# Decoder trunk on one core: half of the down projection's low weight halves formed by ScalarE and an accumulating DMA

## The chip, the cores and the metric

The kernel runs on one core of one Trainium2 chip. The metric is the device time of one execution in microseconds (us); three runs of the kernel before gave 2397.7 to 2398.99 us, median 2398.13 us. TensorE, VectorE, ScalarE, GpSimd and SyncE stand in the profile as PE, DVE, ACT, POOL and SP.

## The reference

Two identical layers are applied to x, one sequence of 256 tokens with 2048 channels, float32:

```python
for l in range(DEPTH):                       # DEPTH = 2
    h = rms_norm(x, mix_norm_w[l])
    x = x + hybrid_mixer(h, w_in[l], ..., w_out[l])
    h = rms_norm(x, ffn_norm_w[l])
    x = x + swiglu(h, w_gate[l], w_up[l], w_down[l])
return rms_norm(x, final_norm_w)

def swiglu(h, w_gate, w_up, w_down):         # 2048 x 5632, 2048 x 5632, 5632 x 2048
    return (jax.nn.silu(h @ w_gate) * (h @ w_up)) @ w_down
```

The mixer runs three groups of heads (mLSTM, forgetting attention, gated DeltaNet) between two projections. All weights are float32 and each is used once per execution.

## The kernel before

The weights lie in HBM as units of 128 x 1024 float32 (512 KB), 410 of them per layer, in the order in which the program uses them. For each unit, `unit` (L112 to L125) has SP load it into a tile `raw` (three buffers), has ACT write a copy rounded to the fp32r format into `whi` (L123), and has DVE write the rest, `raw - whi`, into `wlo` (L124). `whi` and `wlo` have four buffers each. A product of float32 accuracy is then three fp32r matmuls: high by high, high by low, low by high.

The feed-forward part, `ffn`, cuts its 5632 hidden columns into three parts of 16, 16 and 12 blocks of 128. In each part, for every block, `block_a` multiplies one gate block and one up block (two units each); first all matmuls with `whi` (L157, tiles `pg` and `pu`), then those with `wlo` (L161), so that all four `wlo` buffers are held until the end of a block. Then comes the down projection of the part: `block_b` goes through 32 units (24 in the third part), and each unit serves 12 matmuls of 512 columns in the order `whi`, `wlo`, `whi` for two groups of tokens (L184, L185, L186, tile `dn`). In the third part the last 512 output columns are taken in two stretches of 256 columns, the very last of them in the last layer by `block_b_halves` (L199 to L201). Over both layers there are 176 down units in six entries from gate and up to down.

The order on each engine's queue is set by the scheduler of the tile framework, from its own estimate of the times; buffers are handed on by semaphores. POOL has little to do: powers for the norms (L211), some of the convolution (L472, L475) and memsets. It issues no DMA.

Of the kernel before, what the change touches and what calls it, by code (L numbers as in the profile page):

```python
# [15 lines left out]
AF = mybir.ActivationFunctionType  # L16
ALU = mybir.AluOpType
AX = mybir.AxisListType
MUL, ADD, SUB, MAX = ALU.mult, ALU.add, ALU.subtract, ALU.max
# [40 lines left out]
def tile_trunk(ctx: ExitStack, tc: tile.TileContext, x: bass.AP, wu: bass.AP, prm: bass.AP,  # L60
               cst: bass.AP, fnw: bass.AP, out: bass.AP, depth: int, units: list):
    nc = tc.nc
    act, dve, pe, pool = nc.scalar, nc.vector, nc.tensor, nc.gpsimd
# [33 lines left out]
    def f32(ap):  # L97
        return ap.bitcast(F32)
# [5 lines left out]
    def fetch(desc):  # L104
        u, n = len(units), desc[-1] * desc[-2]
        units.append(desc)
        raw = wp.tile([P, 1024], F32, tag="raw", name="raw", bufs=3)[:, :n]
        nc.sync.dma_start(out=raw, in_=wu[u][:, :n])
        return raw
# [4 lines left out]
    def unit(desc):  # L114

        raw = fetched.pop(desc) if desc in fetched else fetch(desc)
        n = desc[-1] * desc[-2]
        whi = wp.tile([P, 1024], F32R, tag="whi", name="whi")[:, :n]
        wlo = wp.tile([P, 1024], F32R, tag="wlo", name="wlo")[:, :n]
        halves = 2 if desc == FIRST else 1  # L120
        for i in range(halves):
            c = slice(i * n // halves, (i + 1) * n // halves)
            act.activation(out=whi[:, c], in_=raw[:, c], func=AF.Copy)  # L123
            dve.tensor_tensor(out=wlo[:, c], in0=raw[:, c], in1=f32(whi[:, c]), op=SUB)  # L124
        return whi, wlo  # L125


# [20 lines left out]
    def block_a(l, cols, hs):  # L148


        los = []
        for mat, col, ps in cols:
            for half in range(2):
                whi, wlo = unit(("a", l, mat, col, half * 8, 8, P))
                los.append(wlo)
                for i in range(8):
                    pe.matmul(ps, whi[:, i * P:(i + 1) * P], hs[half * 8 + i][2], start=(half + i == 0), stop=False)  # L157
        for n, (mat, col, ps) in enumerate(cols):
            for half in range(2):
                for i in range(8):  # L160
                    pe.matmul(ps[:, :S], los[2 * n + half][:, i * P:(i + 1) * P], hs[half * 8 + i][0],  # L161
                              start=False, stop=(half == 1 and i == 7))
# [9 lines left out]
    def block_b(l, mat, col, pst, hs, k0, kts, first, last, w=512):  # L172

        n = 1024 // w
        for j in range(0, kts, n):
            whi, wlo = unit(("b", l, mat, col, k0 + j, min(n, kts - j), w))
            for i in range(min(n, kts - j)):
                hhi, hlo = hs[j + i][:2]
                w1, w2 = whi[:, i * w:(i + 1) * w], wlo[:, i * w:(i + 1) * w]
                st = first and j + i == 0  # L180
                en = last and j + i == kts - 1
                for t in range(2):
                    sl = slice(t * P, (t + 1) * P)
                    pe.matmul(pst[t][:, :w], hhi[:, sl], w1, start=st, stop=False)  # L184
                    pe.matmul(pst[t][:, :w], hhi[:, sl], w2, start=False, stop=False)  # L185
                    pe.matmul(pst[t][:, :w], hlo[:, sl], w1, start=False, stop=en)  # L186

    def block_b_halves(l, mat, col, pst, hs, k0, kts, w):

        n = 1024 // w  # L190
        ws = []
        for j in range(0, kts, n):
            whi, wlo = unit(("b", l, mat, col, k0 + j, n, w))
            ws += [(whi[:, i * w:(i + 1) * w], wlo[:, i * w:(i + 1) * w]) for i in range(n)]
        for t in range(2):
            sl = slice(t * P, (t + 1) * P)
            for j, (w1, w2) in enumerate(ws):
                hhi, hlo = hs[j][:2]
                pe.matmul(pst[t][:, :w], hhi[:, sl], w1, start=(j == 0), stop=False)  # L199
                pe.matmul(pst[t][:, :w], hhi[:, sl], w2, start=False, stop=False)  # L200
                pe.matmul(pst[t][:, :w], hlo[:, sl], w1, start=False, stop=(j == kts - 1))  # L201
# [725 lines left out]
```

## Time and profile before

| | |
|---|---|
| median of three runs | 2398.13 us |
| the profiled execution's own time | 2399.22 us |
| its span in the trace | 2397.4 us |
| PE busy | 2382.9 us, 99% of the span, granted clock 0.999 |
| DVE busy | 1477.3 us, 62% |
| ACT busy | 1194.7 us, 50% |
| POOL busy | 77.2 us, 3% |
| DMA | 436.11 MB, mean 182 GB/s, SP's queue 55.6% of 16 engines |

Busy time of PE says that a matmul is under way, not that it runs at its peak; but an engine that is busy for 99% of the span leaves almost no gaps for others to fill. The page's chain that ended last gives PE 97% of the span. `dn<-wlo,hid` means an instruction that writes the tile `dn` from `wlo` and `hid`; L124 is line 124 of the kernel. In the rows further down, a bracket with an arrow names what ended the idle time of the engine before the row.

### The profile page before, as it was taken

How to read it: one execution, taken by the hardware profiler on the slowest of the kernel's cores; microseconds unless marked ns; L12 is line 12 of the kernel's file. 1: busy time of each engine (PE TensorE's matmuls, PEld its weight loads, DVE VectorE, ACT ScalarE, POOL GpSimd, SP SyncE). 2: the span in 40 equal slices, each digit the busy share in tenths (PEclk: the TensorE clock that was granted, in tenths of full speed). 3: DMA queues.
4: the chain of work that ended last, by engine and by line, in shares of the span. 5: the costliest groups of instructions: out<-in, count | busy, mean ns of one | idle time of the engine just before them, and what ended most of it. 6: DMA issues, size and time to landing. Idle time of an engine off the chain costs nothing.

```text
span 2397.4 us, 34530 instructions
## 1 busy us (share of the span) xinstructions
PE 2382.9 (99%) x13344; PEld 2081.5 (87%) x13344; DVE 1477.3 (62%) x2246; ACT 1194.7 (50%) x1879; POOL 77.2 (3%) x107
## 2 busy tenths in 40 slices
PE   9999999999999999999999999999999999999998
PEld 8888888888888888888898888889888888888887
DVE  5896655566655655466558865565665556655665
ACT  6754554555434454444567545454544344544544
POOL 0220000000000000000003000000000000000000
PEclk9999999999999999999999999999999999999999
DMA  6554555465555656555655545454656555565564
GB/s 223 170 172 132 162 164 187 165 194 192 193 195 176 196 190 201 185 182 196 191 173 176 176 130 164 164 178 161 193 196 195 194 183 186 194 209 193 185 200 161
DMA packets 120885, 436.11 MB, mean 182 GB/s; under 512 B 13584, under 2 KB 14352, under 8 KB 120720
## 3 DMA queue, kind: packets, MB, share of 16 engines
q1 hardware_dynamic: 120160, 432.75, 55.6%
q8 instruction: 104, 1.70, 0.3%
q10 hardware_dynamic: 560, 1.15, 0.1%
q14 instruction: 61, 0.50, 0.1%
HBM read 431.76 MB, written 2.10 MB: 181 GB/s over the span
## 4 chain that ended last, share of the span: by engine, by line
PE 97%; ACT 1%; DVE 1%; DMA 1%; issue 0%; POOLq 0%; POOL 0%; DVEq 0%; ACTq 0%
PE pu L157 13%; PE pg L157 13%; PE pu L161 7%; PE pg L161 7%; PE dn L186 7%; PE dn L184 7%; PE dn L185 7%; PE wo L184 2%; PE wo L186 2%; PE wo L185 2%; PE fq L157 2%; PE fk L157 2%; PE gkq L157 2%; PE fk L161 1%; PE fq L161 1%; PE mk L157 1%
## 5 line engine op out<-in xcount | busy, mean ns | idle before, releaser
L124 DVE TENSOR_TENSOR wlo<-raw,whi 128x1024 fp32r<-128x1024 f32 (+2 forms) x821 | 990.6, 1217 | 654.7 <-ACT whi L123 429.3
L123 ACT ACTIVATE whi<-raw 128x1024 fp32r<-128x1024 f32 (+2 forms) x821 | 866.1, 1055 | 900.6 <-DMA raw<-wu 479.8
L157 PE MATMUL pu<-hl,whi 128*128 128x512 f32 x1408 | 350.2, 391 | 0.0
L157 PE MATMUL pg<-hl,whi 128*128 128x512 f32 x1408 | 336.9, 391 | 0.0
L157 PEld LDWEIGHTS pu<-hl,whi 128*128 128x128 f32 x1408 | 259.0, 188 | 50.3
L157 PEld LDWEIGHTS pg<-hl,whi 128*128 128x128 f32 x1408 | 259.0, 188 | 50.2
L185 PE MATMUL dn<-wlo,hid 128*128 128x512 f32 (+1 forms) x728 | 275.9, 379 | 0.0
L186 PE MATMUL dn<-whi,hid 128*128 128x512 f32 (+1 forms) x728 | 275.6, 379 | 0.0
L184 PE MATMUL dn<-whi,hid 128*128 128x512 f32 (+1 forms) x728 | 274.1, 379 | 0.0
L161 PEld LDWEIGHTS pg<-hl,wlo 128*128 128x128 f32 x1408 | 191.0, 190 | 13.1
L161 PE MATMUL pg<-hl,wlo 128*128 128x256 f32 x1408 | 195.1, 282 | 0.0
L161 PE MATMUL pu<-hl,wlo 128*128 128x256 f32 x1408 | 183.3, 283 | 0.0
L161 PEld LDWEIGHTS pu<-hl,wlo 128*128 128x128 f32 x1408 | 175.4, 192 | 0.2
L185 PEld LDWEIGHTS dn<-wlo,hid 128*128 128x128 f32 x728 | 137.0, 188 | 25.7
L186 PEld LDWEIGHTS dn<-whi,hid 128*128 128x128 f32 x728 | 136.9, 188 | 25.6
L184 PEld LDWEIGHTS dn<-whi,hid 128*128 128x128 f32 x728 | 136.6, 188 | 25.0
L184 PE MATMUL wo<-whi,yhl 128*128 128x512 f32 (+1 forms) x320 | 112.5, 353 | 0.0
L185 PE MATMUL wo<-wlo,yhl 128*128 128x512 f32 (+1 forms) x320 | 111.9, 350 | 0.0
L186 PE MATMUL wo<-whi,yhl 128*128 128x512 f32 (+1 forms) x320 | 111.0, 348 | 0.0
L820 DVE TENSOR_TENSOR hid<-up,hid 128x256 fp32r<-128x256 f32 x88 | 37.4, 424 | 90.5 <-ACT hid L819 90.5
L165 ACT COPY up<-pu 128x256 f32<-128x256 f32 x88 | 32.9, 373 | 111.5 <-PE pu L161 111.5
L157 PE MATMUL fk<-hl,whi 128*128 128x512 f32 x256 | 67.8, 401 | 0.0
(362 smaller groups left out, 2879.8 us busy)
## 6 DMA issues: line engine op xcount, KB each, us to landing
raw<-wu SPq DMA_DIRECT2D x808, 512.0 KB, 4.1
raw<-wu SPq DMA_DIRECT2D x10, 420.0 KB, 3.1
xall<-x SPq DMA_DIRECT2D x3, 512.0 KB, 8.3
fw<-fnw SPq DMA_DIRECT2D x2, 512.0 KB, 4.7
out<-xall ACTq DMA_DIRECT2D x2, 512.0 KB, 3.0
out<-xall SPq DMA_DIRECT2D x2, 512.0 KB, 3.0
xall<-x SPq DMA_DIRECT2D x2, 256.0 KB, 4.5
cst<-cst SPq DMA_DIRECT2D x1, 286.0 KB, 2.9
```

What stands on the lines that cost most here:

```text
L123: act.activation(out=whi[:, c], in_=raw[:, c], func=AF.Copy)
L124: dve.tensor_tensor(out=wlo[:, c], in0=raw[:, c], in1=f32(whi[:, c]), op=SUB)
L157: pe.matmul(ps, whi[:, i * P:(i + 1) * P], hs[half * 8 + i][2], start=(half + i == 0), stop=False)
L161: pe.matmul(ps[:, :S], los[2 * n + half][:, i * P:(i + 1) * P], hs[half * 8 + i][0], start=False, stop=(half == 1 and i == 7))
L165: act.copy(out=dst, in_=ps[:, S:])
L184: pe.matmul(pst[t][:, :w], hhi[:, sl], w1, start=st, stop=False)
L185: pe.matmul(pst[t][:, :w], hhi[:, sl], w2, start=False, stop=False)
L186: pe.matmul(pst[t][:, :w], hlo[:, sl], w1, start=False, stop=en)
L820: dve.tensor_tensor(out=lo, in0=up, in1=f32(hi), op=SUB)
```

## The change

Every unit has a running number; `len(units)` is that number plus one when `unit` goes on after the fetch. For down units with an even running number the tile `wlo` is formed in another way: ACT writes the rounded weights with their sign turned into `wlo`, and POOL issues a DMA that reads the unit once more from HBM and adds it onto `wlo`. The first unit of each of the six down stretches is one of these. 88 of the 176 down units are changed.

```diff
             act.activation(out=whi[:, c], in_=raw[:, c], func=AF.Copy)
-            dve.tensor_tensor(out=wlo[:, c], in0=raw[:, c], in1=f32(whi[:, c]), op=SUB)
+            if desc[2] == "down" and len(units) % 2:
+                act.activation(out=wlo[:, c], in_=raw[:, c], func=AF.Copy, scale=-1.0)
+                pool.dma_start(out=wlo[:, c], in_=wu[len(units) - 1][:, c], accum_op=ADD)
+            else:
+                dve.tensor_tensor(out=wlo[:, c], in0=raw[:, c], in1=f32(whi[:, c]), op=SUB)
```

Lines behind L124 move down by four: L161 becomes L165, L185 becomes L189.

ACT's queue at the first entry from gate and up to down, before. The tiles `whi_6315`, `whi_6333` and `whi_6351` are the first three down units, called u0, u1 and u2 from here on; `ga_6299` and `up_6304` belong to the last block of gate and up.

```order
L123 ACTIVATE whi_6315<-raw_6313 128x1024
L819 ACTIVATE hid_6206<-up_6201 128x256
L123 ACTIVATE whi_6333<-raw_6331 128x1024
L123 ACTIVATE whi_6351<-raw_6349 128x1024
L165 COPY ga_6299<-pg_6209 128x256
L165 COPY up_6304<-pu_6210 128x256
L123 ACTIVATE whi_6369<-raw_6367 128x1024
L812 ACTIVATE ga_6299<-ga_6299 128x256
L123 ACTIVATE whi_6387<-raw_6385 128x1024
L819 ACTIVATE hid_6206<-up_6304 128x256
L123 ACTIVATE whi_6405<-raw_6403 128x1024
```

The same place now, and the stretch behind it (u0 is `whi_6315` with `wlo_6316`, u2 `whi_6352` with `wlo_6353`, u4 `whi_6389` with `wlo_6390`):

```order
L123 ACTIVATE whi_6315<-raw_6313 128x1024
L823 ACTIVATE hid_6206<-up_6201 128x256
L123 ACTIVATE whi_6334<-raw_6332 128x1024
L123 ACTIVATE whi_6352<-raw_6350 128x1024
L125 ACTIVATE wlo_6316<-raw_6313 128x1024
L169 COPY ga_6299<-pg_6209 128x256
L125 ACTIVATE wlo_6353<-raw_6350 128x1024
L169 COPY up_6304<-pu_6210 128x256
L816 ACTIVATE ga_6299<-ga_6299 128x256
L123 ACTIVATE whi_6371<-raw_6369 128x1024
L823 ACTIVATE hid_6206<-up_6304 128x256
L125 ACTIVATE wlo_6390<-raw_6387 128x1024
```

The negated copy of u0 stands behind the high halves of u0, u1 and u2, that of u2 behind the copy of `ga`; from u4 on the negated copy of a unit stands ahead of the unit's own high half, and three ACT instructions serve two units.

POOL's queue around the down stretches of the first layer, before:

```order
L211 TENSOR_TENSOR rf<-rf,mhalf 128x8
L211 TENSOR_TENSOR rstd<-rstd,mhalf 128x2
L359 MEMSET gtk 128x256
L211 TENSOR_TENSOR rstd<-rstd,mhalf 128x2
L391 MEMSET gt_11303 128x256
```

And now:

```order
L215 TENSOR_TENSOR rf<-rf,mhalf 128x8
L215 TENSOR_TENSOR rstd<-rstd,mhalf 128x2
L126 DMA wlo<-wu 128x1024 x16
L363 MEMSET gtk 128x256
L126 DMA wlo<-wu 128x1024 x28
L215 TENSOR_TENSOR rstd<-rstd,mhalf 128x2
L395 MEMSET gt_11347 128x256
```

POOL's instructions keep their order, and the 44 DMAs of the layer stand between the two norms' powers; a memset alone stands among them. In the second layer 44 more stand in a row ahead of the final norm's powers.

## Rows read from the trace of the kernel before

**Rows 1.** The page's first part: busy us, share of the span, instructions.

```profile
PE 2382.9 (99%) x13344; PEld 2081.5 (87%) x13344; DVE 1477.3 (62%) x2246; ACT 1194.7 (50%) x1879; POOL 77.2 (3%) x107
```

**Rows 2.** Waits of PE, whole span: us in total, times, longest us.

```profile
PE xT L245 <- DMA xall<-x: 4.7, 1, 4.7
PE mv L184 <- ACT whi L123: 1.1, 1, 1.1
PE cols L431 <- ACT gt L421: 0.6, 1, 0.6
PE dtp L443 <- DVE bg L317: 0.4, 1, 0.4
```

**Rows 3.** Timeline of ACT inside the first down stretch: start us, us, instruction.

```profile
669.77 1.06 ACT L123 ACTIVATE whi<-raw 128x1024 fp32r<-128x1024 f32 x1 [1.66 <-PE dn L186]
672.49 1.06 ACT L123 ACTIVATE whi<-raw 128x1024 fp32r<-128x1024 f32 x1 [1.66 <-PE dn L186]
```

**Rows 4.** Groups by line and form: busy us, mean ns | idle before.

```profile
L124 DVE TENSOR_TENSOR wlo<-raw,whi 128x1024 fp32r<-128x1024 f32 x807 | 978.1, 1223 | 639.2 <-ACT whi L123 413.9 <-PE pg L161 201.5 <-ACT fo L752 7.3
L123 ACT ACTIVATE whi<-raw 128x1024 fp32r<-128x1024 f32 x807 | 855.2, 1060 | 889.3 <-DMA raw<-wu 479.8 <-PE dn L186 236.9 <-PE wo L186 67.6
```

**Rows 5.** Timeline of PE at the first entry to down.

```profile
644.67 1.35 PE L161 MATMUL pg<-hl,wlo 128*128 128x256 f32 x10
645.86 2.08 PE L161 MATMUL pu<-hl,wlo 128*128 128x256 f32 x16
647.78 0.63 PE L184 MATMUL dn<-whi,hid 128*128 128x512 f32 x2
648.25 0.39 PE L185 MATMUL dn<-wlo,hid 128*128 128x512 f32 x1
...
650.08 0.39 PE L185 MATMUL dn<-wlo,hid 128*128 128x512 f32 x1
650.30 0.39 PE L186 MATMUL dn<-whi,hid 128*128 128x512 f32 x1
650.53 0.61 PE L184 MATMUL dn<-whi,hid 128*128 128x512 f32 x2
```

**Rows 6.** Timeline of DVE at the same entry.

```profile
645.10 2.36 DVE L124 TENSOR_TENSOR wlo<-raw,whi 128x1024 fp32r<-128x1024 f32 x2 [2.18 <-PE pg L161]
```

**Rows 7.** Timeline of ACT at the same entry.

```profile
642.37 1.04 ACT L123 ACTIVATE whi<-raw 128x1024 fp32r<-128x1024 f32 x1
644.59 1.06 ACT L123 ACTIVATE whi<-raw 128x1024 fp32r<-128x1024 f32 x1 [1.18 <-DMA raw<-wu]
646.06 0.37 ACT L165 COPY ga<-pg 128x256 f32<-128x256 f32 x1 [0.41 <-PE pg L161]
```

**Rows 8.** DMA queues and issues in 670 to 730 us: KB each, median us to landing.

```profile
q1 hardware_dynamic: 3168, 11.54, 57.4%
...
raw<-wu SPq DMA_DIRECT2D x22, 512.0 KB, 3.4
```

**Rows 9.** Busy time by stretch: us, each engine, PEclk, DMA share, GB/s.

```profile
6.00:10.00 4.00, 3.15 (x9) 2.58 (x10) 3.41 (x7) 4.00 (x9) 0.00 (x0) 1.00 1.02 405
10.00:14.00 4.00, 4.00 (x16) 3.26 (x15) 3.60 (x8) 3.18 (x8) 0.00 (x0) 1.00 1.05 400
...
665.00:730.00 65.00, 65.00 (x288) 53.81 (x288) 33.01 (x30) 25.18 (x25) 0.00 (x0) 1.00 0.58 194
```

**Rows 10.** Groups of POOL by line and form.

```profile
L472 POOL TENSOR_SCALAR tz<-xc,pr 128x256 f32<-128x256 f32 x24 | 25.4, 1060 | 153.0 <-DVE xc L168 110.8 <-issue 31.8 <-DVE gss L500 5.4
...
L501 POOL TENSOR_TENSOR gr<-gss,mhalf 128x16 f32<-128x16 f32 x2 | 6.4, 3194 | 0.0
```

## The prediction

> **What bounds the kernel now.** I read the page's first part, then PE's waits, then the timeline in the down projection, where the change sits. PE is busy for 2382.9 us of the span of 2397.4 us [rows 1], and the waits of PE on anything that the profile names are four, 6.8 us together, none of them in a down stretch and none on `wlo` [rows 2]. So PE's own queue is the time, and the other engines cost something only where they come late for it. DVE is busy for 62% [rows 1]; taking work off it is worth nothing unless PE waits for it, and it does not.
>
> The reader is to see next how the down stretch is paced. ACT starts one `whi` every 2.72 us, and each start is released by PE's last matmul of the unit four before, which gives the buffer back [rows 3]. A unit thus takes PE 2.72 us, and the forming of the halves runs ahead of PE by as much as four buffers allow. At the entry from gate and up it runs ahead by far less: gate and up hold all four `wlo` buffers until their own low matmuls have run, so DVE can begin the low halves of the first two down units only at 645.10 [rows 6], and PE asks for the first at 648.25 [rows 5].
>
> **The change, part by part.** Durations are from the profiled execution, whose own time is 2399.2 us; that is 1.1 us over the median of 2398.1, so I work out what is added and put it on the median.
>
> *Taken off DVE:* 88 subtractions of 1.22 us [rows 4], 108 us. PE waits for none of them, so I cost this at nothing. The cover is the buffers ahead of PE, which the other 88 subtractions keep.
>
> *Put on ACT:* 88 copies with sign. They have the size of a `whi` copy, so I take its 1.06 us [rows 4]. Three copies in two units are 3.2 us of 5.44 us, so ACT keeps up. Queued behind a negated copy is the unit's own `whi`, which waits for the same unit of PE anyway. At the entry, u0's negated copy stands ahead of the copies out of `pg` and `pu`; that delays them by about 0.6 us, and their hidden block is read last in the stretch.
>
> *Put on POOL and the DMA engines:* 88 adds. Let A be the time from ACT's end to the sum's landing. No add and no POOL DMA is in the trace, so A is bounded. From below: a plain load of the same 512 KB lands 3.4 us after issue in this stretch [rows 8], and an add cannot have less to do. From above I take three parts. First, POOL has to issue it: its instruction of the largest shape takes 1.06 us, its dearest 3.19 us [rows 10]. Second, the add reads the old content of `wlo` as well, one more stream of 512 KB; at the saturated rate of the start, 400 to 405 GB/s [rows 9], that is 1.3 us. Third, loads of the next units share the engines, which are 58% taken [rows 9]: half a load, 0.65 us. I take A = 3.4 + 1.06 + 1.3 + 0.65 = 6.4 us, with the cheap row of POOL, since writing requests is nearer to a pass over a tile than to a power. The range keeps A from 3.4 us up to the cases in the rivals.
>
> The Trainium skill, DMA: Bandwidth & Descriptors, section on the anatomy of a DMA on the gpsimd path, fits such a transfer by 2.0 us and its bytes at 436 GB/s, issue included. An estimate by that page is 3.2 us for 512 KB and 4.4 us with the second stream, which would make the sum below 17 us in place of 29; no run so far shows it, and the 3.4 us of a plain load agree with its first figure.
>
> *In the middle of a stretch* the add is hidden. A changed unit's `wlo` buffer comes round every four units, 10.88 us. In that time PE reads it for about 2.05 us (first `wlo` matmul at 648.25, the one behind the last at 650.30 [rows 5]), ACT fills it in 1.06 us, and I leave 0.2 us for hand-overs, so A may be up to 7.5 us before PE waits. The DMA engines, too: two units now ask for two loads and an add of two streams, 4 x 1.3 = 5.2 us of 5.44 us. That is tight, but it fits. A load may take 5.8 us (three `raw` buffers are 8.16 us, less two copies), 2.4 us more than now. Behind an add on POOL's queue there is only the next add, due 5.44 us later, and one memset.
>
> *At the entry* it is not hidden; this is the wait that the change adds. Before, DVE began u0's low half at 645.10 [rows 6] and PE had no wait. Now ACT must finish the high half of u2 first (644.59 + 1.06 = 645.65 [rows 7]), then the negated copy (646.71), then the add. PE wants it at 648.25, its third down matmul. The cover is 1.54 us, so PE stands for A - 1.54 = 4.9 us. Everything behind it on PE moves by that, and PE has nothing to take it back with. u2's add is issued at about 648.2 and wanted 5.4 us after PE got u0's: covered. u4's is wanted three units after u0 ends: covered up to the 7.5 us above. All three parts of both layers begin with a changed unit, so there are six such entries.
>
> Sum: 6 x 4.9 = 29 us. 2398 + 29 = **2427 us**, 1.2% slower. With A = 3.4 it is 6 x 1.86 = 11 us, 2409 us.
>
> **The rivals.**
>
> *The DMA engines become the bound.* An add might cost the engines three passes (in, in, and a sum written apart) and not two. Then two units ask for 5 x 1.3 = 6.5 us, 1.06 us more than PE's 5.44, over 88 pairs 93 us; A grows to 7.7 us and the six entries cost 37 us. 93 + 37 = 130 us, **2528 us**. For it: the engines are at 58% already, and two streams would leave only 4%. Against it: the start of the kernel shows over 400 GB/s held for 8 us [rows 9]. It decides from 2.2 passes on. The Trainium skill, Collectives: The Full Stack, section on the bandwidth ceiling, says that a reduction in a DMA engine reads two sources and so runs at half a copy's rate, the sum itself being free. By that rule it is two passes and this rival does not come; no row here shows an add.
>
> *POOL is slow to issue.* If writing the requests takes as long as POOL's dearest row, 3.19 us, A is 3.4 + 3.2 + 1.3 + 0.65 = 8.5 us. The entries cost 6 x 7 = 42 us, and in the middle the buffer comes round 1.0 us late per four units: some 38 times outside the entries, 38 us. Together 80 us, **2478 us**. For it: POOL's rows are uneven. Against it: a DMA request touches no 128 x 1024 elements.
>
> *Not slower.* The sum lands within 2.3 us of ACT's end, so that an entry costs under 0.8 us and six under 4.8: **2398 to 2403 us**. The place is u0's low half and the point is A = 2.3 us. Against it stands the 3.4 us of a plain load. For it only that part of the 3.4 us may be waiting behind other loads. A true gain would need PE to win back idle time, of which there are 14.5 us in all [rows 1], none of it behind the subtractions.
>
> **How the numbers follow.** The forecast (A from 3.4 to 7.5 us, the middle hidden, 2409 to 2434 us) has 0.51; the DMA engines as the bound 0.28, in less or more than the worked size; POOL slow 0.17; not slower 0.04. The range goes from 2409 to 2530 us: it leaves out the 0.04 below and some 0.12 above, an add dearer than three passes. About 0.2%, 4.8 us, is what a measurement of this kernel tells from no change. Slower by more than that: 0.95, within it 0.04, faster 0.01.
>
> **What would show each step.** Right: PE has six waits on a DMA before `dn<-wlo` of 4 to 6 us, each at the first unit of a stretch; between them ACT still starts a unit's copies in PE's pace of 2.72 us; DVE has 88 subtractions fewer; the bytes read rise by 88 x 524288 = 46 MB; the granted clock stays. Wrong towards the DMA engines: their share near full in the down stretches, `raw` landing after 6 us and more, PE's pace above 2.72 us throughout. Wrong towards POOL: POOL busy for over 3 us per add with the DMA share low. The prediction falls if no wait of PE stands at the entries, or if most of the loss lies in the middle.

## The result and the profile after

The changed kernel takes 2502.76 us (median of four runs, 2499.14 to 2510.62) against 2398.53 us for the kernel before on the same chip. The ratio is 1.044, interval 1.0428 to 1.0452. The change costs 104 us; the forecast was 29 us, with the right sign. (2502.76 us lies inside the stated range only because the range was drawn up to 2530 us to take in the full engines, whose cause is not the one found below.) The profiled execution took 2501.83 us, its span is 2500.1 us, and its rows stand for the median within 1 us.

First the changed kernel's page: part 1 (busy us, share of the span, instructions), the queues of part 3 (packets, MB, share of 16 engines), the chain by engine, three groups (line, engine, count, busy us, mean ns, idle before them), and two DMA issues (KB, us to landing).

```profile
PE 2407.8 (96%) x13344; PEld 2085.6 (83%) x13344; DVE 1376.2 (55%) x2158; ACT 1278.8 (51%) x1967; POOL 153.4 (6%) x195
...
q1 hardware_dynamic: 120160, 432.75, 51.5%
q0 software_dynamic: 12672, 46.14, 10.3%
...
PE 76%; DMA 11%; issue 10%; ACT 2%; DVE 1%; POOLq 0%; POOL 0%; DVEq 0%; ACTq 0%
...
L189 PE MATMUL dn<-wlo,hid 128*128 128x512 f32 (+1 forms) x728 | 287.1, 394 | 78.0 <-DMA wlo<-wu 77.6
...
L126 POOL DMA_DIRECT2D wlo<-wu x88 | 76.6, 875 | 1458.5 <-ACT ga L169 833.8
...
L125 ACT ACTIVATE wlo<-raw 128x1024 fp32r<-128x1024 f32 x88 | 93.2, 1060 | 127.5 <-PE dn L189 125.3
...
raw<-wu SPq DMA_DIRECT2D x808, 512.0 KB, 4.3
wlo<-wu POOLq DMA_DIRECT2D x88, 512.0 KB, 8.4
```

The moved work is exactly what the forecast counted: 88 subtractions fewer on DVE (2246 instructions before [rows 1], 2158 now), 88 copies of 1.06 us more on ACT, 88 requests of 0.87 us on POOL, 46.14 MB more to read. The one row that is far off is the last: an add lands 8.4 us after its issue (median; 6.6 to 12.4 us). And PE, which waited for almost nothing before [rows 2], now waits for it:

```profile
PE dn L189 <- DMA wlo<-wu: 77.6, 38, 9.2
PE xT L249 <- DMA xall<-x: 4.5, 1, 4.5
```

(PE's waits over the whole span: us in total, times, longest.) The first changed unit of each of the six down stretches carries one long wait; these six are 48.2 us of the 77.6 (8.89, 6.42, 7.81, 7.71, 9.17 and 8.2); the other 32 waits are 29.4 us. The first of them looks like this in the timeline of PE (start us, us, instruction, idle before it):

```profile
646.31 0.63 PE L188 MATMUL dn<-whi,hid 128*128 128x512 f32 x2
655.83 0.80 PE L189 MATMUL dn<-wlo,hid 128*128 128x512 f32 x1 [8.89 <-DMA wlo<-wu]
656.43 0.63 PE L190 MATMUL dn<-whi,hid 128*128 128x512 f32 x1
656.85 0.63 PE L189 MATMUL dn<-wlo,hid 128*128 128x512 f32 x1
...
658.99 0.42 PE L188 MATMUL dn<-whi,hid 128*128 128x512 f32 x1
659.24 0.40 PE L189 MATMUL dn<-wlo,hid 128*128 128x512 f32 x1
659.48 0.40 PE L190 MATMUL dn<-whi,hid 128*128 128x512 f32 x1
```

and in the timelines of ACT and of POOL, which feed it:

```profile
643.96 1.06 ACT L123 ACTIVATE whi<-raw 128x1024 fp32r<-128x1024 f32 x1 [1.76 <-DMA raw<-wu]
644.93 1.04 ACT L125 ACTIVATE wlo<-raw 128x1024 fp32r<-128x1024 f32 x1
...
649.50 1.06 ACT L123 ACTIVATE whi<-raw 128x1024 fp32r<-128x1024 f32 x1 [1.74 <-DMA raw<-wu]
```

```profile
646.30 2.07 POOL L126 DMA_DIRECT2D wlo<-wu  x2 [175.49 <-ACT ga L169]
```

The negated copy ends at 645.97, POOL starts the request 0.33 us later, and PE gets the sum at 655.83: A, from ACT's end to the sum, is 9.86 us here. PE asked at 646.94 (655.83 less 8.89), 0.97 us after ACT's end. So 9.86 - 0.97 = 8.89 us, the forecast's own formula with A = 9.86 for 6.4 and a cover of 0.97 for 1.54.

PE then goes on slowly: from 655.83 to 659.24 it starts eight matmuls in 3.41 us, 0.43 us apart, where the kernel before has one every 0.23 us [rows 5]. That is 1.6 us more. The windows of the changed kernel show the clock beside it (start and end, length in us, then busy us of PE, PEld, DVE, ACT, POOL, granted clock, DMA share, GB/s):

```profile
646.00:655.00 9.00, 0.94 (x6) 0.51 (x5) 3.68 (x7) 3.12 (x6) 1.95 (x2) 0.84 0.77 228
656.00:659.50 3.50, 3.50 (x10) 2.73 (x11) 0.00 (x0) 0.00 (x0) 0.00 (x0) 0.57 0.86 235
672.00:735.00 63.00, 58.72 (x250) 45.93 (x248) 16.37 (x16) 31.53 (x31) 9.57 (x11) 1.00 0.98 258
```

After nearly nine idle microseconds the granted clock is 0.57, close to the lower level of 1.2 GHz, and in 660 to 664 us it is back at 1.00. Behind the other five entries it is 0.50 to 0.53 in the first 3.5 us after the wait.

The third window is the middle of the stretch. It held 0.58 and 194 GB/s before [rows 9] and holds 0.98 and 258 GB/s now, with PE busy for 58.72 of 63 us. The timeline of ACT gives the pace there, by two negated copies twelve pairs of units apart:

```profile
665.15 1.06 ACT L125 ACTIVATE wlo<-raw 128x1024 fp32r<-128x1024 f32 x1 [1.38 <-PE dn L189]
...
675.43 1.06 ACT L123 ACTIVATE whi<-raw 128x1024 fp32r<-128x1024 f32 x1 [2.60 <-DMA raw<-wu]
...
738.40 1.06 ACT L125 ACTIVATE wlo<-raw 128x1024 fp32r<-128x1024 f32 x1 [1.09 <-PE dn L189]
```

73.25 us for 24 units is 3.05 us a unit against 2.72 [rows 3]. A negated copy waits for PE to give a `wlo` buffer back; a `whi` copy now often waits for its load (18.2 us in nine waits between 672 and 735 us), where before it waited only for PE.

Split by place: the first six units of the four full stretches take 27.28, 24.82, 25.88 and 27.85 us, 16.35 us each before, and units six to thirty run at 3.07, 3.03, 2.92 and 3.20 us instead of 2.72. With the two shorter stretches that is some 60 us at the entries and some 45 us in the middle. The forecast had the first, at half its size, and nothing of the second.

### The profile page after: what moved, and what is told of

Its sections match the earlier page's. It is cut to its first block, busy times and chain, and to the rows that moved or that the text cites. A ratio compares the mean times of both kernels' runs of the same rounds, so it can differ in the third digit from the quotient of the medians.

```text
span 2500.1 us, 34715 instructions
## 1 busy us (share of the span) xinstructions
PE 2407.8 (96%) x13344; PEld 2085.6 (83%) x13344; DVE 1376.2 (55%) x2158; ACT 1278.8 (51%) x1967; POOL 153.4 (6%) x195
## 3 DMA queue, kind: packets, MB, share of 16 engines
q0 software_dynamic: 12672, 46.14, 10.3%
## 4 chain that ended last, share of the span: by engine, by line
PE 76%; DMA 11%; issue 10%; ACT 2%; DVE 1%; POOLq 0%; POOL 0%; DVEq 0%; ACTq 0%
DMA wlo<-wu 10%; PE pg L161 10%; PE pu L161 10%; PE pg L165 5%; PE pu L165 5%; PE dn L189 4%; PE dn L190 4%; PE dn L188 3%; PE wo L188 2%; PE fq L161 2%; PE wo L190 2%; PE wo L189 2%; PE fk L161 2%; PE gkq L161 2%; PE fk L165 1%
## 5 line engine op out<-in xcount | busy, mean ns | idle before, releaser
L128 DVE TENSOR_TENSOR wlo<-raw,whi 128x1024 fp32r<-128x1024 f32 (+2 forms) x733 | 883.5, 1217 | 802.6 <-ACT whi L123 560.1
L189 PE MATMUL dn<-wlo,hid 128*128 128x512 f32 (+1 forms) x728 | 287.1, 394 | 78.0 <-DMA wlo<-wu 77.6
L161 PE MATMUL pu<-hl,whi 128*128 128x512 f32 x1408 | 350.2, 391 | 0.0
L161 PE MATMUL pg<-hl,whi 128*128 128x512 f32 x1408 | 336.9, 391 | 0.0
L161 PEld LDWEIGHTS pu<-hl,whi 128*128 128x128 f32 x1408 | 259.0, 188 | 50.3
L161 PEld LDWEIGHTS pg<-hl,whi 128*128 128x128 f32 x1408 | 259.0, 188 | 50.2
L189 PEld LDWEIGHTS dn<-wlo,hid 128*128 128x128 f32 x728 | 140.3, 193 | 124.0 <-DMA wlo<-wu 98.3
L165 PEld LDWEIGHTS pg<-hl,wlo 128*128 128x128 f32 x1408 | 191.0, 190 | 13.1
L165 PE MATMUL pg<-hl,wlo 128*128 128x256 f32 x1408 | 195.1, 282 | 0.0
L165 PE MATMUL pu<-hl,wlo 128*128 128x256 f32 x1408 | 183.3, 283 | 0.0
L165 PEld LDWEIGHTS pu<-hl,wlo 128*128 128x128 f32 x1408 | 175.4, 192 | 0.2
L126 POOL DMA_DIRECT2D wlo<-wu x88 | 76.6, 875 | 1458.5 <-ACT ga L169 833.8
L190 PEld LDWEIGHTS dn<-whi,hid 128*128 128x128 f32 x728 | 140.0, 192 | 25.1
L188 PEld LDWEIGHTS dn<-whi,hid 128*128 128x128 f32 x728 | 138.7, 191 | 26.5
L125 ACT ACTIVATE wlo<-raw 128x1024 fp32r<-128x1024 f32 x88 | 93.2, 1060 | 127.5 <-PE dn L189 125.3
L189 PE MATMUL wo<-wlo,yhl 128*128 128x512 f32 (+1 forms) x320 | 111.9, 350 | 0.0
```

The lines of the kernel that those rows point to most:

```text
L125: act.activation(out=wlo[:, c], in_=raw[:, c], func=AF.Copy, scale=-1.0)
L126: pool.dma_start(out=wlo[:, c], in_=wu[len(units) - 1][:, c], accum_op=ADD)
```

## The experiments

The questions: is it the DMA alone, or also the copies on ACT? Why does an add take 8.4 us: its second stream, other adds, its bytes, or loads that go ahead of it? And is the middle bound by full DMA engines (the rival) or by buffers that come round late? All edits are to the changed kernel; each run is compared with the kernel before on its own chip, 2397.88 to 2398.15 us.

**The add left out.** The add's line goes, the negated copy stays.

```diff
                 act.activation(out=wlo[:, c], in_=raw[:, c], func=AF.Copy, scale=-1.0)
-                pool.dma_start(out=wlo[:, c], in_=wu[len(units) - 1][:, c], accum_op=ADD)
```

> ScalarE's negated copy stays, POOL's DMA is left out, so the low half of 88 units is minus the rounded weights. If the DMA add alone makes the loss (both theories: engines full, and the buffer loop), the time is that of the kernel before, 2396 to 2402 us, and no wait of PE stands before L189. If the copies on ScalarE or their order carry part of it, more than 2405 us.

Measured: 2398.52 us, ratio 1.0001, interval 0.9992 to 1.0011. The copies on ACT cost nothing, and 101 us less work on DVE (1376.2 us busy in this run) give nothing. All 104 us are the DMA's.

**A plain load in the add's place.** The same bytes from memory, on the same queue, without the read of `wlo`.

```diff
-                pool.dma_start(out=wlo[:, c], in_=wu[len(units) - 1][:, c], accum_op=ADD)
+                pool.dma_start(out=wlo[:, c], in_=wu[len(units) - 1][:, c])
```

> POOL's DMA writes the weights over wlo and does not add (the low half of 88 units is the whole weight). The same issue path, one pass less. If the second read of an add is what makes it long, the DMA lands after 5 to 6.5 us instead of 8.4, the DMA share in the middle of a down stretch falls from 0.98 to about 0.85, the middle is back at 2.72 us per unit, and only the entries cost: 6 x (4 to 6) us, 2422 to 2436 us. If the path over POOL is what makes it long, it lands after 8 us and the time stays near 2495 us.

Measured: 2448.28 us, 1.0218 (1.02 to 1.0236), somewhat over what was expected. It lands after 5.9 us (median of all 88; 5.0 in the middle of the first stretch), where a load on SP's queue took 3.4 us in that stretch before the change [rows 8]. Six entries still wait 2.6 to 6.3 us, and the middle is nearly back at 2.76 to 2.79 us a unit. So the second stream is worth 54 us of the 104; the other 50 stay with a plain load in its place. The queues of this run and of the changed kernel, each over its middle (672 to 737 and 670 to 735 us), give the packets' time for one:

```profile
q1 hardware_dynamic: 3303, 12.04, 50.8%
q0 software_dynamic: 1719, 6.26, 33.7%
```

```profile
q1 hardware_dynamic: 3048, 11.11, 49.7%
q0 software_dynamic: 1541, 5.60, 47.7%
...
raw<-wu SPq DMA_DIRECT2D x22, 512.0 KB, 6.2
wlo<-wu POOLq DMA_DIRECT2D x11, 512.0 KB, 8.4
```

In the changed kernel SP's queue takes 0.497 x 65 us for 11.11 MB, 1.52 us of all engines for each 0.524 MB; the adds take 0.477 x 65 us for 5.60 MB, 2.90 us each: 1.9 passes. In the run with plain loads a load on POOL's queue comes to 1.83 us, 1.3 times that run's 1.44 us for a load on SP's queue. The Trainium skill, Collectives: The Full Stack, section on the bandwidth ceiling, has a reduction at half a copy's rate because it reads two sources; the 1.9 agree. Against the plain load on the add's own queue it is 1.6 (2.90 to 1.83), and the packets' time is no fixed price: a load's was 1.57 us before the change (57.4% of 60 us for 11.54 MB [rows 8]).

**The first and third changed unit of a stretch by DVE again.**

```diff
-            if desc[2] == "down" and len(units) % 2:
+            first = desc[2] == "down" and desc[3] == 0 and desc[4] % 16 < 8
+            if desc[2] == "down" and len(units) % 2 and not first:
```

(The two are u0 and u2, the first and third unit of the stretch.)

> The first and the third unit of each down stretch go back to VectorE; 76 adds stay. If entries and middle are two separate losses, the six long waits (48 us, and about 10 us of slow clock behind them) go and the middle's 45 us stay: 2435 to 2450 us. If the wait only moves on to the first add that is left, 2480 us and more.

Measured: 2474.24 us, 1.032 (1.0304 to 1.0335). A miss: the first waits are gone, but now u4's add makes PE wait 2.9 to 3.6 us in each stretch, and the middle stays at 2.99 to 3.11 us. The total lies between the two accounts. A later start moves part of the wait to the next add.

**Five `wlo` buffers.** The space comes from `pt` and `p2` in the mixers (one buffer each).

```diff
-        wlo = wp.tile([P, 1024], F32R, tag="wlo", name="wlo")[:, :n]
+        wlo = wp.tile([P, 1024], F32R, tag="wlo", name="wlo", bufs=5)[:, :n]
```

> Five buffers for wlo in place of four (two mixer tiles give up their second buffer). Loop theory (an add lands 8.4 us after issue, and a buffer that must come back every four units, 10.88 us, allows 7.5): with 13.6 us to come round the middle is back at 2.72 us per unit, and u0's add starts a buffer earlier: 2398 to 2415 us. Full-engines theory (two loads and an add take the 16 DMA engines 5.95 us, PE 5.44 us): the middle still runs at about 2.98 us per unit and costs 35 to 45 us, 2435 to 2455 us.

Measured: 2486.06 us, 1.0371 (1.0356 to 1.0387), outside both ranges: a miss. The first wait falls to at most 1.5 us, since the negated copy no longer needs the buffers of gate and up; u2's add takes its place with 5.0 to 5.6 us. The middle hardly moves (3.07, 3.01, 2.93 and 3.00 us, for 3.07, 3.03, 2.92 and 3.20). ACT's waits in this run, 672 to 735 us, name the load before both kinds of copy:

```profile
ACT whi L123 <- DMA raw<-wu: 13.9, 6, 4.3
ACT wlo L125 <- DMA raw<-wu: 11.2, 6, 4.2
```

Either the engines are full, or the loads' own three buffers are now what comes late. This run leaves that open; a later one decides it.

**One unit in four.** 44 adds in place of 88.

```diff
-            if desc[2] == "down" and len(units) % 2:
+            if desc[2] == "down" and len(units) % 4 == 1:
```

> Every fourth down unit is changed and not every second: 44 adds, beginning with the third unit in the first layer's stretches and with the first unit in the second layer's. Full-engines theory: four loads and an add need 4 x 1.52 + 2.90 = 9.0 us of the engines in PE's 10.88, so the middle is back at 2.72 us per unit; what is left are the entries of the second layer, 3 x (5 to 9) us, and less than 3 us each in the first: 2415 to 2435 us. Loop theory (a buffer comes round every four units and an add takes 8.4 us): 0.9 us per add stays, some 40 us more: 2450 us and above.

Measured: 2465.42 us, 1.0283 (1.0268 to 1.0298). The DMA share in 672 to 735 us is 0.81, an add still lands in 7.6 us, and the middle takes 2.81 to 2.92 us a unit. Entries wait 3.46 to 4.14 us where u2 is the first changed unit and 6.16 to 7.7 us where it is u0. The total is where the loop account put it (2450 us and above), but the middle loses 0.1 to 0.2 us a unit and not the 0.23 of that account, and the first layer's entries wait longer than the 3 us of the other. With half as many adds an add is nearly as long: most of its length does not come from other adds.

**A quarter of the bytes.** Only 256 of 1024 columns are added.

```diff
-                pool.dma_start(out=wlo[:, c], in_=wu[len(units) - 1][:, c], accum_op=ADD)
+                q = slice(0, 256)
+                pool.dma_start(out=wlo[:, q], in_=wu[len(units) - 1][:, q], accum_op=ADD)
```

> The DMA adds only the first 256 of 1024 columns (the other low halves stay minus the rounded weights). If an add's time goes with its bytes, the engines need 2 x 1.52 + 0.73 = 3.8 us of 5.44, the middle is back at 2.72 us per unit, an add lands after 3.5 to 4.5 us, and the six entries cost 2 to 4 us each: 2410 to 2424 us. If most of the 8.4 us is a fixed cost of POOL's path, it lands after 6.5 us and more: above 2430 us.

Measured: 2448.25 us, 1.0213 (1.0196 to 1.023). The middle is back at 2.72 us, with 4.5 us to landing in the median, as the first account had it. The entries are not, and they take the total past that account's 2424 us:

```profile
PE dn L190 <- DMA wlo<-wu: 32.9, 6, 6.3
```

A quarter of the bytes leaves 5.5 us of wait on average, two thirds of the changed kernel's 8.0. Most of the wait at an entry does not go with the add's bytes.

**Six adds only.** Only u0 of each stretch is changed.

```diff
-            if desc[2] == "down" and len(units) % 2:
+            if desc[2] == "down" and desc[3] == 0 and desc[4] % 16 == 0:
```

> Only the first unit of each of the six down stretches is changed, six adds in all. If an add alone, with no other add beside it, is short, it lands after 6 to 7 us and the entries cost 6 x (4.5 to 6.5) us with the slow clock behind the wait: 2425 to 2437 us. If the entry's price is that of the full change, 8 us of waiting and 1.7 us of slow clock: 2450 to 2458 us. The middle runs at 2.72 us per unit in both cases.

Measured: 2459.26 us, 1.0252 (1.0237 to 1.0267). That is just above the second account. Six adds of 88 cost 61 us, 59% of the whole loss; the middle is at 2.72 us. The waits of PE over the span, then the DMA queues from 645.6 to 650 us, where POOL starts the first add at 645.71, and from 650 to 653.5 us (packets, MB, share; for an issue KB, us to landing):

```profile
PE dn L189 <- DMA wlo<-wu: 47.7, 6, 8.6
```

```profile
q1 hardware_dynamic: 268, 1.00, 72.2%
...
raw<-wu SPq DMA_DIRECT2D x3, 512.0 KB, 5.0
wlo<-wu POOLq DMA_DIRECT2D x1, 512.0 KB, 9.3
```

```profile
q0 software_dynamic: 121, 0.50, 73.6%
q1 hardware_dynamic: 79, 0.29, 21.5%
```

Up to 650 us SP's queue moves 1.00 MB, with three loads issued in that time, and POOL's queue not one packet. Then 0.50 MB of the add go through in 3.5 us, and the sum lands some 1.5 us later, at 655.0. So with no other add in the kernel, 4.3 of the 9.3 us pass before its first packet.

The loads that go ahead were not under way when the add was issued: no queue moves a packet from 645.0 to 646.2 us. SP began to issue one 0.3 us before POOL started and one 0.1 us after it, and was done with both by 646.23, while POOL's request lasts until 646.78 (645.71 and 1.07 us). All six adds of this run show the same: the first packet comes 4.3 to 4.5 us after POOL's start, when 0.98 to 1.04 MB, two loads, have gone ahead. The run of the one in four has the case without: the second add of each of its six stretches meets empty queues, and its first packet comes 1.6 us after POOL's start, with 6.9 to 7.1 us to landing. The first such add, in POOL's timeline:

```profile
661.97 0.87 POOL L126 DMA_DIRECT2D wlo<-wu  x1 [13.16 <-ACT wlo L125]
```

Its first packet is at 663.56. So 1.6 of the 4.3 to 4.5 us pass with no load in the way, and the other 2.8 go with the two loads. Behind the wait, the windows of the run with six adds show the clock as in the changed kernel:

```profile
655.00:660.00 5.00, 4.97 (x14) 4.00 (x15) 0.00 (x0) 0.64 (x1) 0.00 (x0) 0.63 0.12 50
660.00:670.00 10.00, 10.00 (x45) 8.26 (x44) 4.90 (x4) 3.60 (x4) 0.00 (x0) 1.00 0.48 159
```

61.4 us less 47.7 us of waits leaves 2.3 us an entry, most of it this (1.8 us in the first, by the pitch of the matmuls).

**The third unit by DVE.** Only u2 goes back, to see whether the second add, issued together with the first, delays it.

```diff
-            if desc[2] == "down" and len(units) % 2:
+            third = desc[2] == "down" and desc[3] == 0 and desc[4] % 16 == 4
+            if desc[2] == "down" and len(units) % 2 and not third:
```

> Only the third unit of each stretch goes back to VectorE, 82 adds. If the first add waits long because the third unit's add, issued 1.2 us behind it, shares the engines with it, the first wait of each stretch falls from 8 to 5.5 us: 2480 to 2490 us. If not, 2497 to 2506 us.

Measured: 2503.37 us, 1.0437 (1.0421 to 1.0452), as the changed kernel. The first waits are still 7.7 to 8.1 us. The second add is not the cause of the first wait.

**Four `raw` buffers.** `wlo` keeps four; the space again from `pt` and `p2`.

```diff
-        raw = wp.tile([P, 1024], F32, tag="raw", name="raw", bufs=3)[:, :n]
+        raw = wp.tile([P, 1024], F32, tag="raw", name="raw", bufs=4)[:, :n]
```

> All 88 adds, four buffers for raw, four for wlo. If in the changed kernel itself the wlo loop or the full engines bind, the middle stays at 3.0 us per unit and the time at 2490 to 2505 us. If the raw buffers bind it, the middle falls to 2.8 us and the time by 15 us and more.

Measured: 2473.57 us, 1.032 (1.0304 to 1.0335), 29 us better than the changed kernel, as the account of the `raw` buffers had it. Entries wait about as long as in the changed kernel (5.9 to 9.7 us), the middle falls to 2.77 to 2.90 us a unit. An add lands after 7.0 us in the median, for 8.4; no run shows why it got shorter.

**Both: four `raw`, five `wlo`.** All 88 adds; `qk`, `xc` and `rb` of the mixers go to one buffer as well.

```diff
-        raw = wp.tile([P, 1024], F32, tag="raw", name="raw", bufs=3)[:, :n]
+        raw = wp.tile([P, 1024], F32, tag="raw", name="raw", bufs=4)[:, :n]
...
-        wlo = wp.tile([P, 1024], F32R, tag="wlo", name="wlo")[:, :n]
+        wlo = wp.tile([P, 1024], F32R, tag="wlo", name="wlo", bufs=5)[:, :n]
```

> All 88 adds, five buffers for wlo and four for raw (mixer tiles give up second buffers). Five wlo buffers alone left the middle at 3.0 us per unit with raw landing after 6.5 us, so either the engines are full or the loop has moved to the three raw buffers. Full engines (5.95 us of work for two units): the middle stays at 2.95 to 3.0 us, in all 2470 to 2490 us. Loop over raw: with four buffers the middle is back at 2.72 to 2.76 us, in all 2435 to 2455 us.

Measured: 2434.94 us, 1.0154 (1.0139 to 1.0169): 68 of the 104 us back, the total of the account of the `raw` buffers without its pace of 2.72 to 2.76. The first waits at the entries are 1.6 to 3.7 us, the middle takes 2.79 to 2.86 us. The middle window of the run with four `raw`, and of this one:

```profile
672.00:735.00 63.00, 61.16 (x268) 49.98 (x268) 17.60 (x17) 34.14 (x34) 9.91 (x12) 1.00 1.02 284
```

```profile
672.00:735.00 63.00, 61.41 (x267) 49.19 (x266) 17.57 (x17) 33.02 (x32) 8.72 (x10) 1.00 1.00 279
```

With one more load buffer the same engines move 284 GB/s, with both 279, and not the 258 of the changed kernel at a share of 0.98. So that share was no ceiling: what bounded the middle were buffers that came round late. Which buffers, the four runs together say: a fourth `raw` buffer lowers the middle with four `wlo` buffers (2.92 to 3.20 us, then 2.77 to 2.90) and with five (2.93 to 3.07, then 2.79 to 2.86), while a fifth `wlo` buffer leaves it where it is in both cases. In the two runs with four `raw` buffers the engines may be full; the last 0.1 us of a unit above 2.72 would fit that, and no run shows it apart.

**One unit in four, five `wlo`.** Two earlier edits together.

```diff
-        wlo = wp.tile([P, 1024], F32R, tag="wlo", name="wlo")[:, :n]
+        wlo = wp.tile([P, 1024], F32R, tag="wlo", name="wlo", bufs=5)[:, :n]
...
-            if desc[2] == "down" and len(units) % 2:
+            if desc[2] == "down" and len(units) % 4 == 1:
```

> Every fourth unit changed, five buffers for wlo. With four buffers the middle ran at 2.81 to 2.92 us per unit although the engines were taken for only 0.81. If that was the buffer coming round (1.06 + 0.3 + 7.6 + 2.3 = 11.3 us against 10.88), 13.6 us cover it: 2.72 us per unit, and 2405 to 2435 us with what the entries keep. If the adds cost PE's feed something else, 2.8 us stays and the time is above 2445 us.

Measured: 2437.05 us (2423.43 to 2439.3), 1.0151 (1.0124 to 1.0179), just above the first account. The rows are of an execution of 2423.43 us, the lowest of the four and 13.6 us under the median. In them the DMA share is 0.84, entries wait up to 3.1 us, the middle takes 2.78 to 2.89 us. That is the pace of the second account: a fifth `wlo` buffer does not bring the middle back here either, so in these rows the `wlo` loop is not what holds it above 2.72.

**The same, with no add at an entry.** A unit is changed only where its loop over the output columns is past the first (`desc[3]` not 0); 33 adds are left.

```diff
-            if desc[2] == "down" and len(units) % 2:
+            if desc[2] == "down" and len(units) % 4 == 1 and desc[3]:
```

> Every fourth unit changed, five buffers for wlo, and none of the first eight units (six in the third part) of a stretch: 33 adds. If entry and buffer loop are all that an add costs below full engines, the adds are hidden: 2397 to 2404 us, no faster than before, since the work taken off VectorE was in nobody's way. If a rest is left (load traffic, ScalarE's order), 2410 us and more.

Measured: 2413.52 us, 1.0066 (1.0049 to 1.0083). The entries are clean: six units take 16.35 us as before the change. But 15 us remain, 11.8 us of them in twelve waits for an add: some 10 us over the first account, as the second had it (2410 us and more). One of the late adds in the timelines of ACT and POOL:

```profile
2143.83 1.06 ACT L123 ACTIVATE whi<-raw 128x1024 fp32r<-128x1024 f32 x1 [3.79 <-DMA raw<-wu]
2144.89 1.06 ACT L125 ACTIVATE wlo<-raw 128x1024 fp32r<-128x1024 f32 x1
```

```profile
2146.24 0.86 POOL L126 DMA_DIRECT2D wlo<-wu  x1 [11.48 <-DVE wlo L128]
```

ACT waits 3.79 us for the load that this copy reads. SP began to issue that load 0.8 us after the add before it (POOL's start at 2133.90); it landed after 9.0 us. So this add starts 12.34 us after the one before and not 10.88, and lands after 9.3 us. In this place an add has slowed a load, and the slow load has made the next add late. The first packet of these 33 adds comes 1.7 to 3.1 us after POOL's start with one load, 0.45 to 0.53 MB, ahead of it, once 5.0 us with two. Work on VectorE does not hold the packet back at this add: behind the start at 2146.24 VectorE does nothing until the packet comes, 2.6 us later.

No run measured alone what the mixers lose by single `pt` and `p2` buffers. In this run's trace it is nothing that shows: the first down stretch begins at 646.53 us, before the change at 647.78 [rows 5]. No version here is faster than the kernel before.

## Why the prediction was right or wrong

**Right: what bounds, and what is free.** PE's queue is the time. DVE's relief and ACT's 88 copies are worth nothing, as costed: 2398.52 us without the adds. POOL's request takes 0.87 us, 1.06 was put, so the rival of a slow POOL falls. Its 2478 us came nearer than the forecast by luck: it had an add of A = 8.5 us, for another reason.

**Right: the entry.** There are six waits, each at the first changed unit of a stretch, and each is A less the cover. The cover was 0.97 us in the first, for 1.54.

**Wrong: A, the step on which the sum rests.** The forecast put 6.4 us. Measured are 8.4 us from issue to landing in the median, 8.5 to 9.3 us for six adds alone, and 9.86 us from ACT's end at the first entry. Two terms were too small. The half load put for traffic, 0.65 us, is two whole loads at an entry: the add has no packet for 4.3 to 4.5 us while 0.98 to 1.04 MB go ahead, 2.8 us longer than on empty queues. Neither other adds (six alone wait 47.7 us, the full 88 wait 48.2 us there) nor mostly its bytes (a quarter of them still 32.9 us) make that time. The second stream, put at 1.3 us, is 2.5 us in time to landing, 8.4 less the plain load's 5.9; in the packets' time it is 2.90 less 1.52, 1.4 us, near what was put. With the six waits of the trace the same formula gives 48 us at the entries instead of 29. By the Trainium skill, DMA: Bandwidth & Descriptors, section on the anatomy of a DMA on the gpsimd path, the estimate was 3.2 to 4.4 us; the 8.4 us here do not agree, nor do the 6.9 us of an add that meets empty queues (loads issued behind it share the engines).

**Wrong: "the granted clock stays".** In the 3.5 us after each entry's wait it was 0.50 to 0.57. By the pitch of the matmuls this is 1.6 us in the first; an estimate for six from it is some 10 us. The forecast had charged a stall by its length alone.

**Wrong: the middle hidden.** The forecast set two limits and held both terms to be inside them. A might be up to 7.5 us and is 8.4: the loop over four `wlo` buffers is then 1.06 us of copy, 0.33 us to POOL, 8.4 us of add, 2.05 us of reading and 0.2 us, 12.0 us or 3.0 us a unit, and 3.05 is measured. A load might take 5.8 us (8.16 less two copies is 6.04; the rest is the 0.2 us for hand-overs) and takes 6.2. By these sums both loops come late. The runs bear out only the second: the fourth `raw` buffer brought the middle down, the fifth `wlo` buffer did not, with either number of `raw` buffers. That the first sum meets 3.05 shows nothing by itself; with four `raw` buffers A falls to 7.0 us and the same loop fits. The prediction said that it would fall if most of the loss lay in the middle. That is 45 of 104 us, just under half, so this sign did not come; the forecast failed by the size of the entries and by leaving the middle out.

**The rival of the full engines** gave 2528 us, close by number only. It asked for three passes and they are 1.9. The share of 0.98 looked like it, and four `raw` buffers moved a tenth more through the same engines (284 for 258 GB/s). The forecast's own 5.2 us of engine time for two units is not borne out either: in the run with four `raw` buffers, at a share of 1.02, the packets take 5.65 us of all engines for two loads and an add (from the two rows below), where PE needs 5.44. So a small part of the middle, the 0.1 us a unit that is left there, may be the engines after all; the packets' time is no fixed price, so this stays open.

```profile
q0 software_dynamic: 1620, 5.87, 51.4%
q1 hardware_dynamic: 3305, 11.99, 50.0%
```

**Open.** Why loads that are issued around POOL's start go ahead of the add whole was not varied: no run held loads back at an entry. What is left of an entry's wait with five `wlo` buffers, and the 0.1 us a unit in the middle of the runs with one add in four, have no cause shown.

## What to carry to other kernels

A DMA that takes an engine's place in a chain costs its time from issue to landing in the busiest moment that it meets, with the loads that are issued around it; here a quiet load's 3.4 us was a floor far below the 8.5 to 9.3 us of six adds alone. Look for the place with the least cover, here the entry of a stage: six adds of 88 made 59% of the loss. Then check every ring of buffers whose period the new transfer enters, and above all the rings of the loads that it slows, before calling the engines full: a share of 0.98 still had a tenth of bandwidth in it. A sum that meets the measured pace does not name the ring; one more buffer in each ring by turns did. And relief for an engine that nobody waits for was worth nothing (ratio 1.0001).

## What the hardware showed that was not expected

- The first packet of an add on POOL's queue came 1.6 us after POOL's start on empty queues, 1.7 to 3.1 us after it with one load ahead, and 4.3 to 4.5 us after it with two, though SP began to issue one of these 0.1 us after POOL's start. A quarter of the columns, in all units, landed after 4.5 us in the median.
- An add's packets took 1.9 times the engine time of a load of the same size on SP's queue, a plain load on POOL's queue 1.3 times.
- After waits of 6.4 to 9.2 us PE's granted clock was 0.50 to 0.57 in the next 3.5 us, with matmuls 0.43 us apart and not 0.23.
- The DMA engines' share did not say what was left: 258 GB/s at 0.98 became 284 GB/s at 1.02 with one more load buffer.
